# Two of three token groups share the weight chunks of an output projection in a two-layer encoder kernel

## The chip, the cores and the metric

The kernel runs on one core of a Trainium2 chip. The metric is the device time of one execution in microseconds (us). The engines of a core are TensorE (PE; PEld is its weight load), VectorE (DVE), ScalarE (ACT), GpSimd (POOL) and SyncE (SP), which here issues nearly all DMAs.

## What is computed

An encoder trunk of two layers and a final RMSNorm, on a prompt of 1024 tokens and a sample of 512, width 1024, in float32. Cut to what matters:

```python
def attn_retention_layer(x, g, w_in, qk_gain, ret_decay, w_out):      # layer 0
    z = rmsnorm(x, g) @ w_in
    ...        # oa: attention over all tokens, 8 heads on 2 kv heads; ob: retention, 4 heads
    mixed = jnp.concatenate([jax.nn.silu(ga) * oa, jax.nn.silu(gb) * ob], axis=-1)
    return x + mixed @ w_out

def windowed_layer(x, g, w_in, sink, rel_bias, w_out):                # layer 1
    ...        # o: attention in a window of +-128 tokens, 16 heads on 2 kv heads
    return x + (jax.nn.silu(gate) * o) @ w_out

def trunk(x, ...):
    x = attn_retention_layer(x, ...)
    x = windowed_layer(x, ...)
    return rmsnorm(x, final_norm)
```

`trunk` is applied to the prompt and to the sample with the same weights. The change concerns the two lines `x + ... @ w_out`.

## The kernel before

**Groups and operands.** The 12 blocks of 128 tokens form three groups of 512 (`NG`, `GB`): t=0 and t=1 are the prompt's halves, t=2 is the sample. The order of work is `ORDER = (2, 0, 1)`. Each float32 operand of a projection is held as a high and a low part (`split`: high part on ACT, low part on DVE), and one step of a projection is three matmuls, high by high, low by high and high by low. The width of 1024 is cut into eight slices of 128, numbered k; `X["h", k, t]` and `X["l", k, t]` are the parts of slice k of group t.

**Weights.** `load_w` (L130) loads one chunk of 256 output columns: four DMAs of 256 KB into raw buffers (two in all), for each a copy to the high part on POOL (L136) and a subtraction for the low part (L137) on POOL or, where `lo` is given, on DVE. Parts go into four buffers of the tag "w" or four of the tag "wg". The "wg" buffers also serve `stage` (L250), from which come the tiles of the mixes (`mo`), of the residual (`y`), of the reloaded rows (`yn`) and of the norm (`dg`).

**Two forms of output projection.** `out_proj_fm` (L263) works with features on the partitions and the weights stationary: per chunk two blocks of 128 features, each 8 steps k of three matmuls 128x512. Behind each block come the residual add on DVE (L278), a store of the result to memory, the square on ACT (L280) and the accumulation on POOL (L282). At its end matmuls with ones give the sums of squares and a tile `R` that holds the row factors of the norm for every partition (L288 to L295), and a last pass reloads every stored block and finishes it (`fin`, L301): in layer 0 by `fin_fm` (L804: multiplication on POOL, then `split_x`), in layer 1 by `fin_out` (L1006: one DVE step and the output store). `out_proj` (L316) works with tokens on the partitions: per chunk four blocks of tokens, each 8 steps of three matmuls 128x256, the residual add in place (L326); it loads its own weights with high priority, odd chunks into "wg" buffers. Its finish is `fin_ab` (L842: norm per block, transposes, splits) or `fin_c` (L1033: norm per block on ACT, POOL and DVE, and stores).

**The mixes.** `mix_fm` (L254) makes the input of a projection: it loads an attention output and a gate, multiplies them on POOL (L259) and splits the product. The last slices of a group are mixed directly at the end of their attention unit (`Back.mix`, L661).

**What sets the order.** Attention A and attention C run through `pipeline` (L673), unit by unit (group of heads, token block), group t=2 first; the scores of later units run beside the products of the current one. After every key block the pipeline calls `fill.step()`, which advances a generator of other work by a rate (`Fill`, L229; `FillC`, L899); a step is three matmuls. `hook_a` (L810) and `hook_c` (L1012) are called once per unit and put output projections into the filler as soon as their group's attention is complete: in both layers t=2 at the first unit of t=0, then t=0 at the first unit of t=1; inside the projection each block advances the mixes of the next group by one (`ahead`). The projection of t=1 follows after attention as `out_proj`. So each of the two output weights is loaded three times. A scheduler that simulates a timeline (L1129) then orders the instructions of each engine within the data's dependencies and the priorities.

## Time and profile before

| | |
|---|---|
| runs, us | 1539.06, 1546.78, 1547.49; median 1546.78 |
| span of the profiled execution, us | 1541.9 |
| PE busy | 1467.9 us, 95% |
| PEld, DVE, ACT, POOL busy | 83%, 69%, 46%, 52% |
| DMA | 179.54 MB, mean 116 GB/s |
| out weights | 48 loads of 256 KB for layer 0, 48 for layer 1 |

The span holds, in this order: input projections and retention, attention A with filler (to 831 us), the rest of projection AB (to 875 us), the projections and attention C with filler (to 1429 us), projection C and the final norm. A share of busy time is a mean over all of these. A busy PE is counted with overlaps, since matmuls are pipelined; the price of one in a row is read from the chain of waits.

### The profile page before, as it was taken

The page shows a single profiled execution, that of the slowest core. Times are in us where ns is not written, and L with a number is a line of the kernel's source. Part 1 is how long each engine was busy: PE and PEld are TensorE (multiplying, and loading weights), DVE is VectorE, ACT ScalarE, POOL GpSimd, SP SyncE. Part 2 cuts the span into 40 slices and gives each one's busy share as a digit, 9 for nine tenths or more (in the row PEclk, how much of TensorE's full clock was granted, in tenths as well). Part 3 has the DMA queues.
Part 4 walks back from the last instruction along what each step waited for, and adds up shares of the span by engine and source line. Part 5 has one row for each costly group of instructions (what it writes and reads, how often), then busy time and mean ns, then how long its engine had stood idle before and what let it go on. Part 6 is the DMA issues. An engine that isn't in the chain of part 4 may idle for free.

```text
span 1541.9 us, 26034 instructions
## 1 busy us (share of the span) xinstructions
PE 1467.9 (95%) x8746; PEld 1277.2 (83%) x8746; DVE 1061.1 (69%) x2488; ACT 714.0 (46%) x1768; POOL 804.7 (52%) x1040
## 2 busy tenths in 40 slices
PE   7989999989999999999998999999999999988897
PEld 7988999987888888778777998888888888766677
DVE  6596455578667667877888327677777767898554
ACT  3632222245455555655653235556556556555102
POOL 7783334257456374887896414442522432567433
PEclk9998999999999999999999999999999999999999
DMA  9441011224421132654563422112213211567773
GB/s 334 155 154 52 19 45 49 64 85 140 138 73 59 48 110 73 217 166 130 153 218 115 124 78 78 52 57 56 80 49 93 61 53 52 169 211 235 242 247 123
DMA packets 112662, 179.54 MB, mean 116 GB/s; under 512 B 12880, under 2 KB 34000, under 8 KB 112528
## 3 DMA queue, kind: packets, MB, share of 16 engines
q1 hardware_dynamic: 110512, 172.37, 35.6%
q0 software_dynamic: 2016, 5.51, 1.2%
q8 instruction: 69, 1.13, 0.3%
q14 instruction: 65, 0.53, 0.1%
HBM read 125.63 MB, written 56.39 MB: 118 GB/s over the span
## 4 chain that ended last, share of the span: by engine, by line
PE 65%; DVE 12%; DMA 8%; POOL 5%; issue 4%; ACT 2%; SPq 1%; POOLq 0%; DVEq 0%; ACTq 0%
PE psg L89 16%; PE psq L89 10%; PE psb L89 8%; PE po L89 8%; PE pte L170 6%; PE pso L89 4%; PE sc L89 3%; PE s L89 3%; PE pskv L89 2%; DMA wraw<-in_woc 2%; DVE xl L118 1%; DVE w L137 1%; DVE nm L782 1%; DMA wraw<-in_woab 1%; DVE el L112 1%
## 5 line engine op out<-in xcount | busy, mean ns | idle before, releaser
L89 PE MATMUL psg<-xh,wg 128*128 128x512 f32 x768 | 261.6, 399 | 1.4 <-POOL wg L137 1.2
L112 DVE TENSOR_TENSOR el<-pte,eh 128x512 fp32r<-128x512 f32 x288 | 196.6, 684 | 56.7 <-ACT eh L111 29.6
L107 POOL TENSOR_SCALAR ec<-ec,rl 128x384 f32<-128x384 f32 (+1 forms) x192 | 109.0, 582 | 233.0 <-DVE rl L997 77.1
L111 ACT ACTIVATE eh<-pte 128x512 fp32r<-128x512 f32 x288 | 169.4, 596 | 119.6 <-PE po L89 66.4
L89 PE MATMUL pso<-xh,w 128*128 128x512 f32 x512 | 179.8, 409 | 9.8 <-DVE w L137 4.3
L89 PEld LDWEIGHTS psg<-xh,wg 128*128 128x128 f32 x768 | 143.7, 188 | 29.7 <-POOL wg L137 1.6
L107 POOL TENSOR_SCALAR e<-e,rl 128x512 f32<-128x512 f32 x160 | 114.6, 728 | 81.7 <-DVE rl L793 23.8
L89 PE MATMUL psg<-xl,wg 128*128 128x512 f32 x384 | 151.1, 393 | 0.0
L992 ACT ACTIVATE ec<-ec,nm 128x384 f32<-128x384 f32 (+1 forms) x192 | 109.6, 572 | 85.6 <-DVE nm L990 80.8
L790 ACT ACTIVATE e<-s,nm 128x512 f32<-128x512 f32 x160 | 108.9, 687 | 75.3 <-DVE nm L787 56.1
L136 POOL TENSOR_SCALAR w<-wraw 128x512 fp32r<-128x512 f32 x116 | 78.7, 680 | 117.7 <-DMA wraw<-in_woc 35.2
L782 DVE TENSOR_REDUCE nm<-s 128x1 f32<-128x512 f32 x160 | 107.5, 682 | 34.3 <-PE s L89 34.0
L89 PE MATMUL psq<-xh,w 128*128 128x512 f32 x384 | 130.1, 397 | 0.6 <-DVE oT L655 0.6
L89 PEld LDWEIGHTS pso<-xh,w 128*128 128x128 f32 x512 | 96.1, 191 | 34.7 <-DVE w L137 7.8
L986 DVE CUSTOM_DVE_ANT_0 ec<-sc,bias,sink_s 128x384 f32<-128x384 f32 (+1 forms) x192 | 105.2, 568 | 20.3 <-PE sc L89 17.4
L89 PE MATMUL pso<-xl,w 128*128 128x512 f32 x256 | 102.0, 399 | 3.3 <-DVE xl L118 3.3
L170 PEld LDWEIGHTS pte<-ident,e 128*128 128x128 f32 x640 | 78.4, 142 | 20.5 <-ACT e L790 1.7
L170 PE MATMUL pte<-ident,e 128*128 128x128 f32 x640 | 94.6, 275 | 0.8 <-ACT e L790 0.6
L137 POOL TENSOR_TENSOR w<-wraw,w 128x512 fp32r<-128x512 f32 x68 | 90.5, 1335 | 1.8
L89 PEld LDWEIGHTS psq<-xh,w 128*128 128x128 f32 x384 | 71.8, 188 | 14.4 <-PE po L89 0.9
L89 PEld LDWEIGHTS psg<-xl,wg 128*128 128x128 f32 x384 | 72.3, 188 | 13.2
L89 PE MATMUL pskv<-w,xh 128*128 128x256 f32 x384 | 73.3, 293 | 9.0 <-ACT xh L117 6.7
(225 smaller groups left out, 3981.8 us busy)
## 6 DMA issues: line engine op xcount, KB each, us to landing
wraw<-in_woab SPq DMA_DIRECT2D x48, 256.0 KB, 3.3
wraw<-in_woc SPq DMA_DIRECT2D x48, 256.0 KB, 3.6
wraw<-in_wab SPq DMA_DIRECT2D x44, 256.0 KB, 3.3
wraw<-in_wc SPq DMA_DIRECT2D x36, 256.0 KB, 3.2
xt<-in_xT SPq DMA_DIRECT2D x24, 256.0 KB, 5.3
xb<-in_x SPq DMA_DIRECT2D x24, 256.0 KB, 4.9
qd<-qdw SPq DMA_DIRECT2D x24, 256.0 KB, 2.0
qd<-qd SPq DMA_DIRECT2D x24, 256.0 KB, 3.1
```

Source lines behind the costliest of these rows:

```text
L89: i = nc.tensor.matmul(ps, lhsT=lhsT, rhs=rhs, start=start, stop=stop)
L107: nc.gpsimd.tensor_scalar(o, i, s, 1.0, ALU.mult, ALU.mult)
L111: nc.scalar.activation(hi, src, AF.Copy)
L112: nc.vector.tensor_tensor(lo, src, hi.bitcast(F32), ALU.subtract)
L118: nc.vector.scalar_tensor_tensor(lo, src, scale, hi.bitcast(F32), ALU.mult, ALU.subtract)
L136: nc.gpsimd.tensor_scalar(w[:, 0, :], raw, 1.0, 1.0, ALU.mult, ALU.mult)
L137: (lo or nc.gpsimd).tensor_tensor(w[:, 1, :], raw, w[:, 0, :].bitcast(F32), ALU.subtract)
L170: return nc.tensor.transpose(o, i, ident)
L782: nc.vector.tensor_reduce(nm2[:, c:c + 1] if nh == 2 else nm[:, h:h + 1], s, AX.X, ALU.max, negate=True)
L790: nc.scalar.activation(eh[c], ss[c], AF.Exp, bias=nm[:, h:h + 1], accum_out=l[:, h, c:c + 1])
L986: nc.vector.tensor_tensor_reduce(es[h][:, :nk], s, bias[h][:, bo:bo + nk], 1.0, sink_s[:, 4 * c + h:4 * c + h + 1], ALU.add, ALU.max, mx[: ...
L992: nc.scalar.activation(es[a][:, :nk], es[a][:, :nk], AF.Exp, bias=nm[:, a:a + 1], accum_out=l[:, a:a + 1])
```

## The change

Only the sample's output projection (t=2) remains filler, in attention A at a rate of 1.15 in place of 2.00. After attention a new function, `out_proj_both`, works on both prompt groups: for each chunk it loads the weights once, with high priority and the low part on DVE, projects two feature blocks of t=0 with weights stationary, then four token blocks of t=1. The results of t=0 stay on the chip until their finish (`ybuf`); in layer 0 they are also stored, as residual for layer 1, in layer 1 they aren't. The norm's sums for t=0 are made after the last chunk's first token block, and the finish of all eight blocks of t=0 (`finish0`) is written ahead of the finish of t=1. The mixes of t=0 and t=1 stay tied to the filler blocks (`aside`), what is left of them is drained at the end of attention. The loads of out weights fall from 48 to 32 per layer.

```diff
+RATE_O = 1.15
...
+    ahead = []
+    def aside():
+        while ahead:
+            if next(ahead[0], aside) is not aside:
+                return
+            ahead.pop(0)
+    def drain():
+        while ahead:
+            aside()
+    def fm_block(w, a, t, k, ks, y, sq, acc, ps):
+        nc.vector.tensor_tensor(y, ps, y, ALU.add)
+        nc.scalar.activation(sq if k else acc, y, AF.Square)
+        if k:
+            nc.gpsimd.tensor_tensor(acc, acc, sq, ALU.add)
+    def fm_rstd(acc, dg, one, rb):
+        nc.gpsimd.memset(one, 1.0)
+        ps = ps_s("ssq")
+        for j in range(GB):
+            mm(ps[:, j:j + 1], acc[:, j * P:(j + 1) * P], one[:, 0:1], True, True)
+        r = rstd_of(ps[:, :GB], D, GB)
+        ps = ps_s("R")
+        for j in range(GB):
+            nc.vector.tensor_scalar(dg[:, j * P:(j + 1) * P], ident, r[:, j:j + 1], None, ALU.mult)
+            mm(ps[:, j * P:(j + 1) * P], one, dg[:, j * P:(j + 1) * P], True, True)
+        nc.scalar.activation(rb, ps, AF.Copy)
...
                     if kk != ks[-1]:
                         yield
-                for side in ahead[:1] + (prev or []):
-                    next(side, None)
-                nc.vector.tensor_tensor(y, ps, y, ALU.add)
+                aside()
+                fm_block(w, a, t, k, ks, y, sq, acc, ps)
                 dma(out=dst[k][t], in_=y)
-                nc.scalar.activation(sq if k else acc, y, AF.Square)
-                if k:
-                    nc.gpsimd.tensor_tensor(acc, acc, sq, ALU.add)
                 yield
...
-        def fin():
-            for k in range(KT):
-                y = stage("yn")[0] if prev is None else buf("Q", "yn")
-                dma(out=y, in_=dst[k][t])
-                finish(t, k, y, rb)
-                yield
-        if prev is None:
-            late.append(fin())
-        else:
-            yield from fin()
-
-    late, ahead = [], []
-
-    def drain(gens):
-        while gens:
-            for _ in gens.pop():
-                pass
-
-    def out_proj(t, warr, ks, res, finish):
-        x1 = [load_block(res(t * GB + j), "xr") for j in range(GB)]
+        for k in range(KT):
+            y = stage("yn")[0]
+            dma(out=y, in_=dst[k][t])
+            finish(t, k, y, rb)
+            yield
+    def out_proj_both(warr, ks, ybuf, res0, keep, finish0, res1, finish1):
+        acc = buf("T", "acc")
+        ys, x1 = [], []
+        def weights(c):
+            with tc.high_priority():
+                return load_w(warr, c, "wg" if c % 2 else "w", nc.vector, None, ks)
+        w = weights(0)
         for c in range(4):
-            with tc.high_priority():
-                w = load_w(warr, c, "wg" if c % 2 else "w", nc.vector, None, ks)
+            for a in range(2):
+                k = 2 * c + a
+                y = ybuf(k)
+                dma(out=y, in_=res0(k))
+                ps = ps_any("pso")
+                for kk in ks:
+                    proj_fm_k(ps, w, a * P, 0, kk, ks)
+                fm_block(w, a, 0, k, ks, y, buf("H", "sq"), acc, ps)
+                keep(k, y)
+                ys.append(y)
+            nxt = weights(c + 1) if c < 3 else None
+            if c == 0:
+                x1 = [load_block(res1(GB + j), "xr") for j in range(GB)]
             for j in range(GB):
                 ps = ps_any("pso")[:, :CW]
-                proj_tm(ps, w, t * GB + j, ks)
+                proj_tm(ps, w, GB + j, ks)
                 sl = x1[j][c // 2][:, (c % 2) * CW:(c % 2 + 1) * CW]
                 with tc.high_priority():
                     nc.vector.tensor_tensor(sl, ps, sl, ALU.add)
-        finish(t, x1)
+                if (c, j) == (3, 0):
+                    rb = buf("T", "rb")
+                    fm_rstd(acc, buf("H", "dg"), buf("O", "one", P), rb)
+            w = nxt
+        for k in range(KT):
+            finish0(0, k, ys[k], rb)
+        finish1(1, x1)
...
     def hook_a(u):
         g, b = u
-        if g == 1 and b in (BLOCKS[GB], BLOCKS[2 * GB]):
-            t = 2 if b == BLOCKS[GB] else 0
-            if t == 2:
-                late.clear()
-                fill.rest()
-                fill.rate = 2.00
-            drain(ahead)
-            if t:
-                drain([mix_fm(t, KS_A, o_ab, g_ab)])
-            ahead.append(mix_fm(0 if t else 1, KS_A[:6], o_ab, g_ab))
-            fill.gens.append(out_proj_fm(t, woab, KS_A, lambda k: xT[k][:, t * 512:(t + 1) * 512], x1T_d, fin_fm,
-                                         None if t else late, None))
+        if g == 1 and b == BLOCKS[GB]:
+            fill.rest()
+            fill.rate = RATE_O
+            ahead.append(mix_fm(2, KS_A, o_ab, g_ab))
+            drain()
+            ahead.append(mix_fm(0, KS_A[:6], o_ab, g_ab))
+            fill.gens.append(out_proj_fm(2, woab, KS_A, lambda k: xT[k][:, 2 * 512:3 * 512], x1T_d, fin_fm, None))
+        if g == 1 and b == BLOCKS[2 * GB]:
+            ahead.append(mix_fm(1, KS_A[:6], o_ab, g_ab))
 
...
-    out_proj(1, woab, KS_A, lambda b: x[b], fin_ab)
+    pairs = {}
+    def y_ab(k):
+        if k >= 6:
+            return buf("S2", "y2")
+        if k % 2 == 0:
+            pairs[k // 2] = buf("S4", "y4")
+        return pairs[k // 2][:, (k % 2) * 512:(k % 2 + 1) * 512]
+    out_proj_both(woab, KS_A, y_ab, lambda k: xT[k][:, 0:512], lambda k, y: dma(out=x1T_d[k][0], in_=y), fin_fm,
+                  lambda b: x[b], fin_ab)
...
     def hook_c(u):
         c, b = u
-        if c == 3 and b in (BLOCKS[GB], BLOCKS[2 * GB]):
-            t = 2 if b == BLOCKS[GB] else 0
+        if c == 3 and b == BLOCKS[GB]:
             for _ in fillc.gates:
                 pass
-            if t == 2:
-                late.clear()
-            drain(ahead)
-            drain([mix_fm(t, KS_C if t else KS_C[6:], o_c, g_c)])
-            ahead.append(mix_fm(0 if t else 1, KS_C[:6], o_c, g_c))
-            fillc.more.append(out_proj_fm(t, woc, KS_C, lambda k: x1T_d[k][t], x2T_d, fin_out, None if t else late, nc.vector))
+            ahead.append(mix_fm(2, KS_C, o_c, g_c))
+            drain()
+            ahead.append(mix_fm(0, KS_C[:6], o_c, g_c))
+            fillc.more.append(out_proj_fm(2, woc, KS_C, lambda k: x1T_d[k][2], x2T_d, fin_out, nc.vector))
+        if c == 3 and b == BLOCKS[2 * GB]:
+            ahead.extend([mix_fm(0, KS_C[6:], o_c, g_c), mix_fm(1, KS_C[:6], o_c, g_c)])
 
...
-    out_proj(1, woc, KS_C, lambda b: x1_d[b], fin_c)
+    out_proj_both(woc, KS_C, lambda k: buf("Q", "y"), lambda k: x1T_d[k][0], lambda k, y: None, fin_out,
+                  lambda b: x1_d[b], fin_c)
```

On POOL at the end of attention A, before (w and wg are weights, acc the sums of squares, yn the reloaded rows, mo a mix, oT an attention output):

```order
L282 TENSOR_TENSOR acc<-acc,y 128x512
L136 TENSOR_SCALAR w<-wraw 128x512
L282 TENSOR_TENSOR acc<-acc,y 128x512
L136 TENSOR_SCALAR wg<-wraw 128x512 x3
L103 TENSOR_TENSOR rstd<-ms,nhalf 128x4
L136 TENSOR_SCALAR wg<-wraw 128x512
L805 TENSOR_TENSOR yn<-yn,rb 128x512 x7
L666 TENSOR_TENSOR oT<-oT,gq 128x256
L136 TENSOR_SCALAR w<-wraw 128x512 x2
```

and after:

```order
L104 TENSOR_TENSOR rstd<-ms,nhalf 128x4
L697 TENSOR_TENSOR oT<-oT,gq 128x256
L836 TENSOR_TENSOR yn<-yn,rb 128x512 x8
L281 TENSOR_TENSOR acc<-acc,sq 128x512
L260 TENSOR_TENSOR mo<-mo 128x512
L697 TENSOR_TENSOR oT<-oT,gq 128x256
L284 MEMSET one 128x128
L260 TENSOR_TENSOR mo<-mo 128x512
L137 TENSOR_SCALAR wg<-wraw 128x512
L260 TENSOR_TENSOR mo<-mo 128x512
L137 TENSOR_SCALAR wg<-wraw 128x512
L260 TENSOR_TENSOR mo<-mo 128x512
```

The eight multiplications `yn` (now the sample's) are followed by mixes of group 1, which before had been made earlier, between filler blocks.

On PE at the same place, before (po is the last product of attention A, pso the projection of group 1, xh and xl the parts of one of its slices):

```order
L89 MATMUL pso_10142<-w_10056,xh71_9755 128x256
L89 MATMUL po_9796<-el_9904,av_7802 128x512
L89 MATMUL pso_10142<-w_10056,xh71_9755 128x256
L89 MATMUL pso_10142<-w_10056,xl71_9756 128x256
L89 MATMUL pso_10214<-wg_10170,xh01_9074 128x256 x2
L89 MATMUL pso_10214<-wg_10170,xl01_9075 128x256
L89 MATMUL pso_10214<-wg_10170,xh11_9216 128x256 x2
L89 MATMUL pso_10214<-wg_10170,xl11_9217 128x256
```

and after:

```order
L90 MATMUL po_9457<-eh_9555,av_7799 128x512
L90 MATMUL po_9457<-el_9556,av_7799 128x512
L90 MATMUL pso_9741<-w_9625,xh01_9243 128x256 x2
L90 MATMUL pso_9741<-w_9625,xl01_9244 128x256
L90 MATMUL pso_9741<-w_9625,xh11_9396 128x256 x2
L90 MATMUL pso_9741<-w_9625,xl11_9397 128x256
L90 MATMUL pso_9741<-w_9630,xh41_9594 128x256 x2
L90 MATMUL pso_9767<-w_9630,xh41_9594 128x256 x2
L90 MATMUL pso_9793<-w_9630,xh41_9594 128x256 x2
L90 MATMUL pso_9741<-w_9630,xl41_9595 128x256
L90 MATMUL pso_9767<-w_9630,xl41_9595 128x256
L90 MATMUL pso_9793<-w_9630,xl41_9595 128x256
```

The number behind a name's h or l tells slice and group: xh41 is the high part of slice 4 of group 1, which comes from the first of the mixes above. Before, the first chunk of group 1 ended beside the last product, one tile after the other, and its second chunk followed; now most of the first chunk stands behind the last product, slice by slice through three tiles.

On DVE at the end of the program, before (xr is a token block of group 1, L326 its residual add, L1037 its last scaling):

```order
L1037 SCALAR_TENSOR_TENSOR xr_17608<-xr_17608,rstd,fn 128x512
L326 TENSOR_TENSOR xr_17612<-pso,xr_17612 128x256
L181 TENSOR_REDUCE ssum<-ss 128x1
L100 TENSOR_SCALAR ms<-ssum 128x1
L1037 SCALAR_TENSOR_TENSOR xr_17612<-xr_17612,rstd,fn 128x512
L326 TENSOR_TENSOR xr_17616<-pso,xr_17616 128x256
L181 TENSOR_REDUCE ssum<-ss 128x1
L100 TENSOR_SCALAR ms<-ssum 128x1
L1037 SCALAR_TENSOR_TENSOR xr_17616<-xr_17616,rstd,fn 128x512
```

and after:

```order
L1073 SCALAR_TENSOR_TENSOR xr_17236<-xr_17236,rstd,fn 128x512
L182 TENSOR_REDUCE ssum<-ss 128x1
L101 TENSOR_SCALAR ms<-ssum 128x1
L1073 SCALAR_TENSOR_TENSOR xr_17240<-xr_17240,rstd,fn 128x512
L1045 SCALAR_TENSOR_TENSOR y<-y,g_sb,rb 128x512 x8
L351 TENSOR_TENSOR xr_17244<-pso,xr_17244 128x256
L182 TENSOR_REDUCE ssum<-ss 128x1
L101 TENSOR_SCALAR ms<-ssum 128x1
L1073 SCALAR_TENSOR_TENSOR xr_17244<-xr_17244,rstd,fn 128x512
```

Eight finishing steps of group 0 (L1045) now stand ahead of the residual add of the last token block.

## Rows read from the trace of the kernel before

**Rows 1.** The page's busy times: engine, microseconds, share of the span, instructions.
```profile
PE 1467.9 (95%) x8746; PEld 1277.2 (83%) x8746; DVE 1061.1 (69%) x2488; ACT 714.0 (46%) x1768; POOL 804.7 (52%) x1040
```

**Rows 2.** Windows: length, busy PE, PEld, DVE, ACT, POOL (instructions), clock, DMA share, GB/s.
```profile
390.00:620.00 230.00, 228.85 (x1171) 189.12 (x1170) 150.36 (x314) 122.13 (x274) 126.34 (x157) 1.00 0.27 81
622.00:831.00 209.00, 198.10 (x1022) 159.04 (x1021) 171.55 (x312) 116.68 (x260) 168.10 (x176) 0.99 0.56 172
1336.00:1429.00 93.00, 81.69 (x379) 63.14 (x379) 84.30 (x178) 46.90 (x117) 66.10 (x71) 0.98 0.69 222
```

**Rows 3.** Waits of PE's weight loads, 635.6 to 809.8: total, times, longest.
```profile
PEld s L89 <- ACT e L790: 3.4, 3, 2.7
...
PEld pte L170 <- issue: 0.2, 1, 0.2
```

**Rows 4.** Timeline of ACT: start, length, evacuation of a unit's accumulator, three units.
```profile
635.64 0.60 ACT L650 ACTIVATE olo<-po 64x512 f32<-64x512 f32 x1
809.82 0.59 ACT L650 ACTIVATE olo<-po 64x512 f32<-64x512 f32 x1
1429.12 0.59 ACT L650 ACTIVATE olo<-po 64x512 f32<-64x512 f32 x1 [3.08 <-PE po L89]
```

**Rows 5.** Windows of the three stretches that are costed, columns as in rows 2.
```profile
635.60:809.80 174.20, 168.12 (x847) 134.62 (x846) 143.68 (x264) 100.96 (x228) 147.38 (x156) 0.99 0.56 171
809.80:875.10 65.30, 58.69 (x440) 55.83 (x439) 40.42 (x68) 19.05 (x45) 36.56 (x39) 0.97 0.40 120
1429.10:1532.40 103.30, 95.20 (x583) 82.98 (x582) 56.67 (x91) 14.54 (x34) 38.85 (x46) 0.97 0.66 207
```

**Rows 6.** The chain of waits: start, length, matmuls of 256 and of 512 columns.
```profile
889.30 26.75 PE pskv L89 x223
936.20 5.49 PE psg L89 x24
```

**Rows 7.** Groups of DVE, 635.6 to 809.8: busy, mean ns, idle before.
```profile
L792 DVE TENSOR_TENSOR rl<-l 128x1 f32<-128x1 f32 x28 | 14.9, 533 | 7.6 <-ACT e L790 7.4
L118 DVE SCALAR_TENSOR_TENSOR xl<-mo,xh 128x512 fp32r<-128x512 f32 x15 | 14.9, 992 | 5.1 <-ACT xh L117 5.0
L278 DVE TENSOR_TENSOR y<-pso,y 128x512 f32<-128x512 f32 x14 | 9.5, 680 | 0.4 <-PE pso L89 0.4
```

**Rows 8.** Groups of POOL in the same stretch.
```profile
L137 POOL TENSOR_TENSOR w<-wraw,w 128x512 fp32r<-128x512 f32 x28 | 38.6, 1380 | 0.3
L136 POOL TENSOR_SCALAR w<-wraw 128x512 fp32r<-128x512 f32 x29 | 18.6, 643 | 6.7 <-PE pso L89 5.2 <-DMA wraw<-in_woab 1.3
L259 POOL TENSOR_TENSOR mo<-mo 128x512 f32<-128x512 f32 x14 | 18.1, 1292 | 4.9 <-DMA mo<-gab 2.5 <-PE pte L170 2.2 <-DMA mo<-oab 0.2
L282 POOL TENSOR_TENSOR acc<-acc,y 128x512 f32<-128x512 f32 x12 | 17.3, 1440 | 5.2 <-DVE rl L793 5.2
L805 POOL TENSOR_TENSOR yn<-yn,rb 128x512 f32<-128x512 f32 x8 | 10.8, 1345 | 2.1 <-DMA yn<-x1T 2.1
```

**Rows 9.** Timeline of POOL at the end of attention A.
```profile
831.33 11.46 POOL L805 TENSOR_TENSOR yn<-yn,rb 128x512 f32<-128x512 f32 x7
```

**Rows 10.** DMA issues on the page: count, KB each, median microseconds to landing.
```profile
wraw<-in_woab SPq DMA_DIRECT2D x48, 256.0 KB, 3.3
```

**Rows 11.** Waits of PE's weight loads in projection C, 1429.1 to 1532.4.
```profile
PEld pso L89 <- POOL w L136: 8.4, 6, 2.5
PEld pso L89 <- DVE w L137: 3.4, 8, 1.0
```

**Rows 12.** Groups of DVE, 1429 to the end.
```profile
L1007 DVE SCALAR_TENSOR_TENSOR yn<-yn,g_sb,rb 128x512 f32<-128x512 f32 x16 | 12.3, 792 | 2.3 <-DMA yn<-x2T 1.2 <-issue 1.1
```

**Rows 13.** Timeline of DVE at the end of the program.
```profile
1533.65 1.74 DVE L1037 SCALAR_TENSOR_TENSOR xr<-xr,rstd,fn 128x512 f32<-128x512 f32 x1 [0.67 <-POOL rstd L103]
1535.32 0.41 DVE L326 TENSOR_TENSOR xr<-pso,xr 128x256 f32<-128x256 f32 x1
```

**Rows 14.** Groups of DVE, 390 to 620.
```profile
L792 DVE TENSOR_TENSOR rl<-l 128x1 f32<-128x1 f32 x31 | 7.9, 254 | 13.5 <-ACT e L790 13.3
```

More of the change, by code (lines that the diff above doesn't have):

```diff
@@ L261, in mix_fm, with out_proj_fm @@
             yield
-    def out_proj_fm(t, warr, ks, res, dst, finish, prev, lo):
+    ahead = []
[23 more added lines that the diff above has]
+        nc.scalar.activation(rb, ps, AF.Copy)
+    def out_proj_fm(t, warr, ks, res, dst, finish, lo):
         acc = buf("T", "acc")
@@ L286, in out_proj_fm @@
-        ps = ps_s("ssq")
-        for j in range(GB):
-            mm(ps[:, j:j + 1], acc[:, j * P:(j + 1) * P], one[:, 0:1], True, True)
-        r = rstd_of(ps[:, :GB], D, GB)
-        ps = ps_s("R")
-        for j in range(GB):
-            nc.vector.tensor_scalar(dg[:, j * P:(j + 1) * P], ident, r[:, j:j + 1], None, ALU.mult)
-            mm(ps[:, j * P:(j + 1) * P], one[:, :P], dg[:, j * P:(j + 1) * P], True, True)
         rb = buf("T", "rb")
-        nc.scalar.activation(rb, ps, AF.Copy)
+        fm_rstd(acc, dg, one[:, :P], rb)
```

9 lines of the change are left out of this document (4 added, 5 removed).

## The prediction

> **What bounds the kernel now.** I read the page's busy times first: TensorE (PE) is busy for 95% of the span, far ahead of VectorE (DVE, 69%), GpSimd (POOL, 52%) and ScalarE (ACT, 46%) [rows 1]. The change leaves the number of matmuls and their sizes as they are, so it can win only where PE waits now, and it loses wherever it makes PE wait anew. Next I cut the span into stages. While attention A is filled with gate projections (390 to 620 us) PE is busy for 228.85 of 230 us and DVE for 0.65 of the time; while it is filled with output projections (622 to 831 us) DVE rises to 0.82 and POOL to 0.80; at the end of attention C, DVE is at 0.91 and PE falls to 0.88 [rows 2]. So the stages with projection filler are where PE is not the only engine near its limit. The list of waits for the seven units of attention A that carry the filler has 11 rows, 13.5 us in all, led by waits for exponentials and splits [rows 3]. The evacuations of the unit accumulator mark the stage: the last sample unit ends at 635.64, the last but one unit at 809.82, and attention C's last unit at 1429.12 [rows 4]. The three stretches to be costed are then 174.2 us (seven units), 65.3 us (from there to the last matmul of projection AB) and 103.3 us (from the end of attention C to the last matmul of projection C) [rows 5].
>
> **Prices.** On the chain of waits, where PE runs without a gap, 24 matmuls of 512 columns take 5.49 us, 0.229 each, and 223 of 256 columns 26.75 us, 0.120 each [rows 6]. The durations in the lists of lines are longer since neighbours overlap, so I don't sum those. A group that is projected with stationary weights needs 8 blocks of 24 matmuls of 512 columns, 44.0 us; the token-major group needs 384 of 256 columns, 46.1 us.
>
> **1. Attention A gets less filler.** By the order of instructions, 128 of group 0's matmuls leave these seven units: 128 x 0.229 = 29.3 us. (Twelve matmuls of 256 columns come in and twelve transposes go, which cancels.) With the waits of 13.5 us [rows 3] held, the stretch goes from 174.2 to 145 us: **-29**. All of this work comes back in step 2. Whether the waits hold is the open point. DVE was busy 143.7 of 174.2 us [rows 5]. It loses, for the group 0 blocks, six adds of 0.68 us and some of the mixes and splits that are now made later (0.99 us each) [rows 7], about 11 us, and would have 132 us of work in 145, a share of 0.91. That is just the share at which attention C already runs [rows 2], so I take the wait as unchanged, and no gain on top. POOL loses far more: of 29 copies of 0.64 us and 28 subtractions of 1.38 us [rows 8] roughly half, besides five accumulations of 1.44: about 36 us, to some 111 of 145.
>
> The Trainium skill, page "Perfetto Trace Analysis", section "Identifying the Most-Contended Engine", would have TensorE judged by the busy share of its weight loads and the others by occupancy. Between 622 and 831 us that is 159.04 of 209 for the loads, 0.76, below DVE's 0.82, so by this rule taking PE work out of the stage buys little. This supports the slower rival below; the 0.95 of matmul time and the 13.5 us of waits speak against it.
>
> **2. End of attention A and projection AB.** Now the stretch is 65.3 us. Moved here are the 29.3 us of step 1, and one new stall. At the end of the last but one unit the sample's R row becomes ready, and POOL's queue then holds, in this order, eight multiplications for the sample's finish, an accumulation and four mixes of group 1, where before the mixes came earlier, beside filler. Before, POOL needed 11.46 us for seven such multiplications [rows 9], with a mean of 1.35 each [rows 8]. From the evacuation: R about +1, its copy +2, eight times 1.35 and a load's delay to +14, an accumulation of 1.44 and a mix of 1.29 [rows 8], then ACT's and DVE's split: PE can begin with the first of these mixes at about +17. Ahead of it PE has only the last unit's remaining transposes and products, some 7 us, so it idles for about **10 us**. The mixes follow at 1.3 to 2 us and the last is there at +24; what is left of chunk 0 then takes 51 x 0.12 = 6 us, to +30. Chunks 1 to 3 need 2 x 24 x 0.229 + 96 x 0.120 = 22.5 us each, and the four loads of a chunk at 3.3 us [rows 10] fit in this. With 2% of small waits: +99.5. Net **+34** against 65.3. Of this 29 is the moved work and 5 the stall, less the 5 us and more that PE waited here before.
>
> **3. Removed loads.** 32 of the 96 weight transfers of 256 KB go, with their copies and subtractions, and the stores and reloads of group 0. In layer A those were hidden by matmuls already, so alone they bring 0. I bound the input projection of layer C, which follows, at -2 to +4 (group 1's transposes start with the same blocks as before) and take 0.
>
> **4. Layer C.** Its filler for group 0 mostly runs after attention already. By the order only 24 matmuls (5.5 us) move out of attention; with DVE at 0.91 there not all of that time is saved: **-4**. After attention there are now 168 matmuls of 512 columns and 384 of 256: 84.6 us of work in 103.3, so PE idles 18.7; 8.4 and 3.4 us of it are waits for the weight copies and subtractions [rows 11], since a token-major chunk of 11.5 us needs four loads of 3.3 and their two conversions. Afterwards a chunk is 22.5 us of work for the same four loads, and these waits should go. There are 90.1 us of work, and I allow 4.5 for chunk 0, which waits for mixes that come after attention, and 2% for the rest: 97. That is -6, **-10** with the 4 above.
>
> **5. The end of the program.** In the order DVE's eight finishing steps of group 0 (y by gain and R) now stand between the last block but one and the last block's residual add. They take 0.79 us each [rows 12]: 6.3 us. Before, that add ran at 1535.32, right behind one finishing step of 1.74 [rows 13], and 6.6 us from there the span ended. The steps can begin only when the step for the block before is through, so most of them is exposed: **+5** (0 if R is ready early and the scheduler's order leaves a gap to hide them, +8 if the eight stores of 256 KB also hold up the last ones).
>
> **Sum**: -29 + 34 + 0 - 10 + 5 = 0 on the profiled span of 1541.9. The median of the runs, 1546.78, lies 4.9 us above that span, so the forecast is **1547 us**. About 0.5%, 7.7 us, is what a measurement of this kernel tells from no change.
>
> **Rivals.**
> (a) *Faster: attention A's waits fall with the load of POOL and DVE.* The pair add of the softmax sums takes 533 ns in the filled units [rows 7] and 254 ns before them [rows 14], and a split 0.99 us; if POOL's smaller share shortens these again, DVE has 28 x 0.28 = 8 us less, some 15 with the splits, and is at 0.87. Then PE's waits go most of the way to those of 390 to 620 us, where it was idle for 1.15 of 230 [rows 2]: with 3.5 us of them left the units take 135 instead of 145, -10. The same shortens the chain of multiplications in step 2 by 4, and in C chunk 0 waits for nothing, -5. In all -19: **1528 us**. The Trainium skill, page "SBUF — State Buffer", section "Who interferes with whom", says the same of the cause: VectorE's instructions with two SBUF inputs and GpSimd's reads exclude each other for whole instructions. The 533 and 254 ns agree with it, though they don't show it alone.
> (b) *Slower: DVE bounds the seven units.* If it can't be filled to more than the 143.7 / 174.2 = 0.825 it has now, its 132 us take 160 instead of 145, +15: **1562 us**. This decides as soon as DVE's waits are latency between engines rather than idleness for lack of PE results; the three waits for exponentials [rows 3] speak for it, attention C's 0.91 [rows 2] against.
> (c) *The sharing doesn't free PE.* Odd chunks go through the four buffers that mixes, staged rows and weights share. If their loads wait until mixes of group 1 are read, 3 us for each of two odd chunks in each layer, PE waits 12 us more than I have: **1559 us**. For it speaks that the first odd chunk is loaded just when the mixes are late (step 2); against, that chunk 0's work covers a load of 3.3 us.
>
> **Chances.** Forecast (within 0.5%) 0.37, (a) 0.33, (b) 0.22, (c) 0.08. Faster by over 0.5% is (a), 0.33; slower is (b) and (c), 0.30. The range goes from (a) with 3 us for an end of the program that costs less, to (b) with 3 more for the stores: 1525 to 1565.
>
> **What would show it.** Right: units of attention A at 20.7 us each; a PE gap of about 10 us between the last product of attention A and the first of the late mixes, with POOL's eight multiplications in it; chunks 1 to 3 of either layer at 22.5 us; waits for weights in layer C's projection down from 12 us to 4 or less; some 14 us from the last projection matmul to the end of the span. Units near 23 us would be (b), near 19.3 (a). If the weight waits in C stay, or odd chunks begin late, it is (c). What would make the forecast wrong most easily is the size of step 1's wait, since 29 us of PE work are taken out of a stage in which DVE is then as full as PE.

## The result

The changed kernel is slower: 1557.53 us in the median of four runs (1551.24 to 1558.83) against 1545.07 (1539.06 to 1547.49), a ratio of 1.0083, 95% interval 1.0055 to 1.0112. That lies in the range of the prediction, but outside the half per cent around its forecast of 1547. The profiled execution was the fastest of the four. The page of the changed kernel, its first lines (as [rows 1]):

```profile
span 1549.5 us, 25836 instructions
...
PE 1466.7 (95%) x8746; PEld 1279.0 (83%) x8746; DVE 1031.5 (67%) x2472; ACT 713.9 (46%) x1768; POOL 761.7 (49%) x992
```

PE has the same work, VectorE 30 us less and GpSimd 43 us less; so the whole loss is time in which PE waits or runs slowly. To find it I cut both traces at the same marks: the evacuation of the last sample unit, that of the last but one unit of attention A, the last matmul of projection AB, the last of layer C's key and value projection, the last evacuation of attention C, the last matmul of projection C, the end. The evacuations in the changed kernel, timeline of ScalarE (as [rows 4]):

```profile
633.98 0.59 ACT L681 ACTIVATE olo<-po 64x512 f32<-64x512 f32 x1
...
781.22 0.59 ACT L681 ACTIVATE olo<-po 64x512 f32<-64x512 f32 x1 [0.81 <-PE po L90]
...
1429.41 0.59 ACT L681 ACTIVATE olo<-po 64x512 f32<-64x512 f32 x1 [0.21 <-DVE oT L686]
```

The stretches between the marks, windows of the changed kernel (length, busy PE, PEld, DVE, ACT, POOL, granted clock, DMA share, GB/s, as [rows 5]):

```profile
634.00:781.20 147.20, 136.05 (x710) 108.53 (x709) 120.96 (x250) 87.96 (x207) 94.45 (x109) 1.00 0.40 123
781.20:886.70 105.50, 95.51 (x584) 84.16 (x584) 43.77 (x72) 26.61 (x57) 51.16 (x52) 0.90 0.39 125
886.70:925.30 38.60, 38.45 (x324) 38.25 (x323) 19.40 (x29) 17.37 (x43) 17.66 (x15) 1.00 0.08 25
925.30:1429.40 504.10, 494.34 (x2523) 414.24 (x2522) 380.40 (x1128) 287.28 (x778) 214.02 (x303) 1.00 0.32 100
1429.40:1536.60 107.20, 97.57 (x606) 88.05 (x605) 41.40 (x76) 18.96 (x46) 38.87 (x40) 0.95 0.37 112
1536.60:1549.50 12.90, 0.05 (x1) 0.00 (x0) 7.71 (x13) 1.66 (x4) 1.01 (x2) 0.66 0.70 261
```

And the three stretches of the kernel before that stand in no row above, in windows:

```profile
875.40:916.10 40.70, 38.75 (x322) 38.31 (x323) 8.16 (x21) 12.15 (x35) 9.71 (x15) 1.00 0.15 46
916.10:1429.10 513.00, 500.77 (x2547) 418.32 (x2546) 390.70 (x1136) 290.27 (x784) 223.82 (x311) 1.00 0.32 100
1532.60:1541.90 9.30, 0.06 (x1) 0.00 (x0) 3.45 (x7) 2.97 (x9) 2.33 (x3) 0.72 0.37 139
```

Beside the prediction's steps, in us (marks read to 0.1 us):

| stretch | before | after | difference | predicted |
|---|---|---|---|---|
| seven units of attention A | 174.2 | 147.2 | -27.0 | -29 |
| rest of attention A and projection AB | 65.4 | 105.5 | +40.1 | +34 |
| key and value projection of C | 40.7 | 38.4 | -2.3 | 0 |
| rest of layer C to the end of attention | 513.2 | 504.3 | -8.9 | -4 |
| projection C | 103.4 | 107.1 | +3.7 | -6 |
| to the end | 9.4 | 13.0 | +3.6 | +5 |
| sum from the last sample unit on | 906.3 | 915.5 | +9.2 | 0 |

Up to the first mark the two kernels issue nearly the same work, and the changed one was there 1.7 us earlier (the last section shows how far runs spread there); this is why the span differs by 7.6 and not by 9.2.

**The end of attention A.** Windows of the changed kernel where PE loses time, at the end of attention A and behind attention C:

```profile
781.20:805.00 23.80, 15.61 (x69) 10.94 (x69) 19.95 (x26) 14.49 (x26) 18.98 (x16) 0.68 0.70 230
805.00:830.00 25.00, 23.20 (x129) 20.31 (x128) 11.93 (x17) 2.32 (x4) 8.93 (x10) 0.90 0.35 96
1429.40:1450.00 20.60, 15.60 (x80) 13.25 (x79) 10.52 (x19) 4.89 (x11) 11.36 (x12) 0.88 0.64 200
1450.00:1475.00 25.00, 22.06 (x123) 19.50 (x124) 12.66 (x19) 2.25 (x4) 7.26 (x8) 0.89 0.67 213
```

From 781 to 805 us PE executes 69 instructions; from 805 to 830 it executes 129. What is ahead of it there, on GpSimd (timeline; the bracket is the idle time before and what ended it):

```profile
784.09 3.85 POOL L836 TENSOR_TENSOR yn<-yn,rb 128x512 f32<-128x512 f32 x3 [0.54 <-ACT rb L293]
788.61 1.27 POOL L836 TENSOR_TENSOR yn<-yn,rb 128x512 f32<-128x512 f32 x1 [0.67 <-DMA yn<-x1T]
791.25 1.57 POOL L836 TENSOR_TENSOR yn<-yn,rb 128x512 f32<-128x512 f32 x1 [1.37 <-DMA yn<-x1T]
793.10 4.74 POOL L836 TENSOR_TENSOR yn<-yn,rb 128x512 f32<-128x512 f32 x3 [0.28 <-DMA yn<-x1T]
797.80 1.71 POOL L281 TENSOR_TENSOR acc<-acc,sq 128x512 f32<-128x512 f32 x1
799.48 1.72 POOL L260 TENSOR_TENSOR mo<-mo 128x512 f32<-128x512 f32 x1
```

The eight multiplications of the sample's finish and then the first late mix, in the predicted order. On VectorE at the same time (timeline), the split of a sample row (L119) stands ahead of each low part (L113) that the last unit's products need:

```profile
786.73 0.68 DVE L113 TENSOR_TENSOR el<-pte,eh 128x512 fp32r<-128x512 f32 x1
787.33 1.16 DVE L119 SCALAR_TENSOR_TENSOR xl<-yn,g_sb,xh 128x512 fp32r<-128x512 f32 x1
788.42 0.68 DVE L113 TENSOR_TENSOR el<-pte,eh 128x512 fp32r<-128x512 f32 x1
789.02 1.41 DVE L119 SCALAR_TENSOR_TENSOR xl<-yn,g_sb,xh 128x512 fp32r<-128x512 f32 x1
```

The waits of PE's weight loads from 781.2 to 830 us (total, times, longest), first the products, then the late mixes:

```profile
PEld po L90 <- DVE el L113: 7.4, 6, 1.8
PEld pso L90 <- ACT xh L118: 5.5, 4, 3.3
```

With two smaller entries these are 13 short waits, 15.3 us in all, where one gap of about 10 us was predicted. By PE's timeline the chunks 1, 2 and 3 begin at 817.7, 840.1 and 862.5 us: the first of them 36.5 us behind the mark, where 30 were predicted, and then 22.4 apart, where 22.5 were. The whole excess is in chunk 0.

**Projection C.** The waits for weights of [rows 11] are gone (0.3 us remain); these stand in their place, from 1429.4 to 1536.6:

```profile
PEld pso L90 <- ACT xh L118: 8.7, 4, 3.0
PEld pso L90 <- DVE y L278: 2.1, 2, 1.5
```

The xh are high parts of late mixes, and GpSimd, which makes the mixes, waits for their loads (timeline):

```profile
1443.57 1.26 POOL L260 TENSOR_TENSOR mo<-mo 128x512 f32<-128x512 f32 x1 [4.35 <-DMA mo<-gc]
...
1453.73 1.27 POOL L260 TENSOR_TENSOR mo<-mo 128x512 f32<-128x512 f32 x1 [2.77 <-DMA mo<-gc]
```

The loads of the last two mixes were issued at 1450.3 and 1451.2 us, right behind the landings of two stores of the sample's rows (1450.3 and 1451.0), which use the same buffers. Chunk 1 begins at 1465.1 us, 35.7 behind the mark, where 27 were allowed for chunk 0.

### The profile page after: what moved, and what is told of

Its sections match the earlier page's. It is cut to its first block, busy times and chain, and to the rows that moved or that the text cites. A ratio compares the mean times of both kernels' runs of the same rounds, so it can differ in the third digit from the quotient of the medians.

```text
span 1549.5 us, 25836 instructions
## 1 busy us (share of the span) xinstructions
PE 1466.7 (95%) x8746; PEld 1279.0 (83%) x8746; DVE 1031.5 (67%) x2472; ACT 713.9 (46%) x1768; POOL 761.7 (49%) x992
## 3 DMA queue, kind: packets, MB, share of 16 engines
q1 hardware_dynamic: 102448, 157.69, 32.1%
## 4 chain that ended last, share of the span: by engine, by line
PE 69%; DVE 11%; POOL 5%; DMA 4%; issue 3%; ACT 2%; SPq 0%; POOLq 0%; DVEq 0%; ACTq 0%
PE psg L90 16%; PE psq L90 10%; PE pso L90 10%; PE psb L90 8%; PE po L90 8%; PE pte L171 6%; PE sc L90 3%; PE s L90 3%; DVE xl L119 1%; PE pskv L90 1%; DVE nm L813 1%; DMA wraw<-in_woc 1%; DVE el L113 1%; POOL mo L260 1%; DVE qdw L431 1%
## 5 line engine op out<-in xcount | busy, mean ns | idle before, releaser
L113 DVE TENSOR_TENSOR el<-pte,eh 128x512 fp32r<-128x512 f32 x288 | 196.4, 684 | 57.4 <-ACT eh L112 29.1
L90 PE MATMUL pso<-xh,w 128*128 128x512 f32 x384 | 136.3, 405 | 2.6 <-DVE w L138 1.4
L1024 DVE CUSTOM_DVE_ANT_0 ec<-sc,bias,sink_s 128x384 f32<-128x384 f32 (+1 forms) x192 | 105.2, 568 | 21.8 <-PE sc L90 18.6
L137 POOL TENSOR_SCALAR w<-wraw 128x512 fp32r<-128x512 f32 x84 | 56.2, 669 | 77.1 <-PE pskv L90 23.3
L90 PEld LDWEIGHTS pso<-xh,w 128*128 128x128 f32 x384 | 72.6, 190 | 17.3 <-DVE w L138 1.9
L171 PE MATMUL pte<-ident,ec 128*128 128x128 f32 x512 | 78.8, 273 | 2.0 <-POOL ec L108 1.9
L90 PE MATMUL pso<-xl,w 128*128 128x512 f32 x192 | 76.2, 397 | 1.9 <-DVE xl L119 1.9
```

The source lines that it names most:

```text
L90: i = nc.tensor.matmul(ps, lhsT=lhsT, rhs=rhs, start=start, stop=stop)
L113: nc.vector.tensor_tensor(lo, src, hi.bitcast(F32), ALU.subtract)
L137: nc.gpsimd.tensor_scalar(w[:, 0, :], raw, 1.0, 1.0, ALU.mult, ALU.mult)
L171: return nc.tensor.transpose(o, i, ident)
L1024: nc.vector.tensor_tensor_reduce(es[h][:, :nk], s, bias[h][:, bo:bo + nk], 1.0, sink_s[:, 4 * c + h:4 * c + h + 1], ALU.add, ALU.max, mx[: ...
```

## The experiments

All stretches in us, read from each trace at the same marks; "A" is the seven units, "AB" the rest to the last matmul of projection AB, "kv" the key and value projection, "C" the rest of layer C to the end of attention, "pC" projection C, "end" the end. The ratio is to the kernel before, with its 95% interval.

| kernel | A | AB | kv | C | pC | end | sum | ratio |
|---|---|---|---|---|---|---|---|---|
| before | 174.2 | 65.4 | 40.7 | 513.2 | 103.4 | 9.4 | 906.3 | |
| changed | 147.2 | 105.5 | 38.4 | 504.3 | 107.1 | 13.0 | 915.5 | 1.0083 (1.0055 to 1.0112) |
| e1 layer A alone | 148.7 | 105.8 | 38.4 | 511.0 | 101.9 | 9.4 | 915.1 | 1.0068 (1.0043 to 1.0093) |
| e2 layer C alone | 174.3 | 64.7 | 40.9 | 506.6 | 106.9 | 13.6 | 907.1 | 1.0007 (0.9992 to 1.0022) |
| e3 early mixes | 150.5 | 93.5 | 38.4 | 510.0 | 98.3 | 13.0 | 903.8 | 0.9979 (0.9963 to 0.9995) |
| e4 finish written last | 148.7 | 105.2 | 38.4 | 502.6 | 106.8 | 13.0 | 914.8 | 1.0077 (1.0047 to 1.0107) |
| e5 early mixes, finish held | 149.4 | 86.9 | 38.4 | 511.0 | 97.0 | 13.0 | 895.8 | 0.9955 (0.9941 to 0.9970) |
| e6 early mixes, not shared | 146.5 | 107.6 | 39.5 | 511.7 | 115.2 | 13.0 | 933.6 | 1.0168 (1.0150 to 1.0185) |
| e7 early mixes, rate 1.60 | 167.0 | 84.0 | 38.4 | 511.5 | 98.1 | 13.0 | 912.1 | 1.0050 (1.0034 to 1.0066) |
| e8 e5, finish split | 148.7 | 87.1 | 38.4 | 510.5 | 96.9 | 14.6 | 896.1 | 0.9953 (0.9938 to 0.9968) |
| e9 e5, blocks forward | 151.4 | 87.1 | 39.1 | 512.2 | 96.8 | 12.7 | 899.2 | 0.9938 (0.9914 to 0.9962) |
| e10 finish held alone | 153.7 | 90.4 | 38.4 | 505.2 | 100.0 | 13.0 | 900.7 | 0.9965 (0.9947 to 0.9982) |
| e11 e9, rate 1.40 | 156.1 | 87.6 | 39.2 | 512.5 | 97.5 | 12.7 | 905.6 | 0.9993 (0.9978 to 1.0008) |
| e12 e9, finish spread | 149.0 | 86.9 | 39.1 | 510.4 | 97.2 | 12.0 | 894.6 | 0.9912 (0.9892 to 0.9932) |

**Which layer loses: e1 and e2.** Each has the new function in one layer, and in the other the old pair with its old hook. The lines are e1's; e2 does the same in layer A.

```diff
-    out_proj_both(woc, KS_C, lambda k: buf("Q", "y"), lambda k: x1T_d[k][0], lambda k, y: None, fin_out,
-                  lambda b: x1_d[b], fin_c)
+    old_proj(1, woc, KS_C, lambda b: x1_d[b], fin_c)
```

> Only projection AB is changed as in the new kernel; layer C stays as in the kernel before. Theory 1 (the traces add up by stretch): attention A's end is where the loss is. In the two traces the new kernel stands 9.2 us behind when the key and value projection of layer C ends and the later stretches give 1.6 back, so this kernel should be about 9 us slower than before (ratio 1.006). Theory 2 (the loss is in layer C's projection and the end of the program, which became 7 us longer in the traces, and layer A's part is given back in layer C): within 2 us of before.

> Only projection C is changed as in the new kernel; layer A stays as in the kernel before. Theory 1: attention C ends 8.8 us earlier relative to its start, the projection takes 3.8 and the end of the program 3.4 us more, so -2 us (ratio 0.999). Theory 2 (the loss sits here): +7 us, ratio 1.005.

Measured: 1.0068 and 1.0007, from the last sample unit on +8.8 and +0.8 us, together 9.6 where both parts at once give 9.2. The parts add up, and layer A carries the loss. In e1 Theory 1 stands, and the 40 us in AB are there unchanged. e2 was to be 2 us faster and isn't, but it is far from the 7 us of Theory 2.

**Whether the late mixes are it: e3.**

```diff
                 aside()
+                aside()
                 fm_block(w, a, t, k, ks, y, sq, acc, ps)
```

> The new kernel with two mixes in place of one for each filler block, so that in layer A none and in layer C two of group 1's mixes are left for the time after attention. Theory 1 (late mixes are what PE waits for at the end of both attentions: 19.3 us of PE waiting from 781 to 830 and 15.2 after 1429 in the new kernel's trace): 8 us less at the end of attention A and 7 less in projection C than the new kernel, so about 1543 us, no slower than before. Theory 2 (at the end of attention A the sample's eight finishing multiplications and splits hold PE up, whether mixes are behind them or not; in projection C the weights take the place of the mixes): at most 4 us less than the new kernel.

Measured: 1541.01 us, 0.9979, as Theory 1 gave, about 16 us below the changed kernel's median. By stretches 3.3 of the 12.0 us that AB gains are lost again in the seven units, into which the mixes went, and in layer C 5.7 of 8.8 in attention; 11.7 remain. Waits were left in e3. At the end of attention A the products still wait for low parts, weight loads from 784.5 to 881 us:

```profile
PEld po L90 <- DVE el L113: 5.2, 4, 2.6
```

and in projection C, from 1429.8 to 1528.2, the first odd chunk is late:

```profile
PEld pso L90 <- POOL wg L137: 4.8, 1, 4.8
```

GpSimd could not copy these weights because the sample's rows, reloaded for their finish, still held the "wg" buffers until they were stored: the first two copies start at 1456.3 and 1457.5 us, 0.2 behind the landings of two of the rows' stores (1456.1 and 1457.3), while their data had landed by 1443.2. That is the mechanism of rival (c), with the sample's rows in the place of mixes; the changed kernel itself doesn't show it since it waits for mixes first.

**The sample's finish: e10 alone, e5 with early mixes.** The reloaded rows of the sample are written behind the first shared chunk, in buffers of the attention's exponentials.

```diff
-            y = stage("yn")[0]
-            dma(out=y, in_=dst[k][t])
-            finish(t, k, y, rb)
-            yield
+        late.append(fin())          # the same four lines with y = buf("E", "yn")
@@ out_proj_both, at the end of each chunk
+            while late:
+                for _ in late.pop():
+                    pass
```

> The new kernel with one mix for a filler block, as it was, and only the sample's finish moved behind the first shared chunk, in buffers of its own. Theory A (at the end of attention A it is the sample's eight multiplications and splits ahead of the mixes that PE waits for): layer A gains as much as in e5, layer C's late mixes stay, so 8 to 10 us less than the new kernel, 1547 to 1549 if before is 1544. Theory B (it is the number of mixes left that counts): at most 3 us less than the new kernel, ratio 1.006 or more.

> The kernel with early mixes (e3), and besides the finish of the sample's rows written behind the first shared chunk in both layers, in buffers that the odd weight chunks don't use. Theory: what is left of the loss is that the sample's rows share buffers and VectorE with what PE waits for: in e3 the first odd chunk of layer C waits 4.8 us until such rows are stored, and the last products of attention A wait 5.2 us for splits that stand behind the sample's. So 5 us less than e3 (about 1536 us), 10 if both go. Rival: the waits of that size in e3 only mask loads that come no sooner, and the time stays within 2 us of e3 (1541).

Measured: e10 0.9965, e5 0.9955. In e10 layer A (A and AB) takes 244.1 us, 8.6 less than the changed kernel, with not one more mix called for in the source: the scheduler placed all of group 1's mixes of layer A ahead of the end of attention (the last at 763.7 us, the mark is at 790.1). That the rows no longer took the buffers that the mixes need is the likely reason; no run tests it alone. So theory B is out, and theory A holds only in part: layer A gains half of e5's 16.4 us, and layer C, where the late mixes were to stay, gains 6.2 in its two stretches (one wait of 5.4 us for a late mix is left there). Since the mixes moved too, e10 doesn't separate the finish from them. e3 alone gives 8.7 in layer A, both together 16.4. In e5 the same place runs without a gap; windows, and GpSimd's timeline, where the multiplications now begin 12 us behind the mark in place of 3:

```profile
786.70:812.00 25.30, 25.30 (x156) 22.20 (x154) 15.82 (x21) 12.09 (x21) 14.71 (x11) 1.00 0.52 165
```

```profile
798.87 5.52 POOL L848 TENSOR_TENSOR yn<-yn,rb 128x512 f32<-128x512 f32 x4 [8.06 <-DMA yn<-x1T]
```

In 25.3 us PE executes 156 instructions at a granted clock of 1.00, where the changed kernel had 69 in 23.8 us at 0.68. Layer A is then 3.3 us shorter than before, layer C's two stretches 8.6.

**Is it the sharing that pays: e6.** As e3, but each chunk is loaded twice, once for each group.

```diff
+            w = weights(c, "wg")
-            nxt = weights(c + 1) if c < 3 else None
+            nxt = weights(c + 1, "w") if c < 3 else None
```

> The kernel with early mixes (e3), but each chunk's weights are loaded twice behind attention, once for group 0 and once for group 1, so nothing is shared and only the place of the projections is changed. Theory 1 (sharing is what makes the chunks of 22.5 us run without waits for weights): eight loads of 3.3 us for a chunk are 26 us, 4 us more than the matmuls, so 20 to 30 us slower than e3 over both layers. Theory 2 (two loads in flight hide each other, sharing brings nothing to PE): within 3 us of e3.

Measured: 1567.97 us, 27 more than e3 (29.8 by the stretches), the number of Theory 1. But its reason holds only in part. Projection C takes 16.9 us more, and it has one wait of 13.6 us where e3's was 4.8, the list of waits from 1438 to 1553 us:

```profile
PEld pso L90 <- POOL wg L137: 13.6, 1, 13.6
```

and it is again a buffer that the sample's rows hold (GpSimd's timeline):

```profile
1464.53 0.62 POOL L137 TENSOR_SCALAR wg<-wraw 128x512 fp32r<-128x512 f32 x1 [9.53 <-DMA out_s<-yn]
```

Layer A's two stretches take 10.1 us more; the longest wait there, 4.6 us, is again for a copy into "wg". So sharing is worth a good deal in this arrangement, but how much of it would be left with buffers of their own was not tried.

**What bounds attention A's units: e7 and e11.**

```diff
-RATE_O = 1.15
+RATE_O = 1.60      # e7, on e3; 1.40 in e11, on e9
```

> The kernel with early mixes (e3) with the sample's projection at a rate of 1.60 in place of 1.15 in attention A: it ends about two units earlier, its finish falls into attention, and the last units run without filler. Theory 1 (the seven units are bound by matmuls): the units with filler grow to 23 us, those without fall to about 16, and the 8.5 us of PE waiting at the end of attention A in e3 shrink, in all 3 to 6 us less than e3. Theory 2 (without filler a unit is bound by VectorE and by latency): those units stay at 18 us or more, PE waits in them, and the kernel is 3 to 6 us slower than e3.

> As e9 with the sample's projection at a rate of 1.40 in place of 1.15. In e7 the units that ran out of filler still took 20.8 to 25 us for 12 us of PE work, so attention A's units have a floor that isn't PE's. Theory (units of about 21 us have room for some 20 us of PE work and hold 17.5 at the rate 1.15): at 1.40 the early units stay within 1 us of 21 and the last ones take group 0's first blocks instead, 3 to 6 us less than e9. Rival (group 0's blocks don't come forward, as in e7): 3 us or more slower than e9.

Measured: 1549.59 and 1542.53 us, each 8 us slower than its base: the direction of Theory 2 with a larger size, and the rival in e11. Windows of e7, a unit with filler and two that have nearly none:

```profile
709.50:731.90 22.40, 21.57 (x112) 17.27 (x111) 18.81 (x40) 13.58 (x33) 15.46 (x18) 1.00 0.44 128
...
759.50:784.70 25.20, 17.89 (x81) 13.54 (x82) 20.86 (x40) 15.34 (x32) 17.30 (x16) 0.86 0.22 68
784.70:805.50 20.80, 15.32 (x85) 11.99 (x84) 17.88 (x36) 11.62 (x27) 12.18 (x15) 0.92 0.48 135
```

With 81 and 85 PE instructions in place of 112 the units take 25.2 and 20.8 us in place of 22.4; at 1.15 they take 21. That looks like a floor of the unit, but isn't shown to be one. The sample's finish runs through both: the longest waits of PE's weight loads there, 3.4 and 3.0 us, are for low parts that stand behind the sample's splits on VectorE, as at the end of attention A in the changed kernel. In e11, where the finish is held, the unit that ran out of filler took 15.2 us, behind one of 25.9 with 153 PE instructions (windows of e11):

```profile
775.40:790.60 15.20, 13.07 (x76) 9.95 (x77) 11.90 (x30) 11.24 (x29) 6.19 (x9) 1.00 0.33 106
```

By the stretches e11 loses 6.4 us to e9: its seven units take 4.7 more, 4.1 of them busy time of PE, and what came forward didn't shorten AB, where PE waits 3.5 us in one piece behind the last unit's output. So a higher rate loses in both kernels; what bounds the units stays open.

**The end of the program: e4, e8, e9, e12.** In the changed kernel, on VectorE's timeline, the eight steps of group 0 and the residual add behind them:

```profile
1537.54 5.38 DVE L1045 SCALAR_TENSOR_TENSOR y<-y,g_sb,rb 128x512 f32<-128x512 f32 x8
1542.84 0.41 DVE L351 TENSOR_TENSOR xr<-pso,xr 128x256 f32<-128x256 f32 x1
```

```diff
-        for k in range(KT):                         # e4: behind finish1, in layer C alone
-            finish0(0, k, ys[k], rb)
         finish1(1, x1)
+        for k in range(KT):
+            finish0(0, k, ys[k], rb)
@@ e8: fin_out
+        if t == 0 and k % 2:
+            nc.gpsimd.tensor_tensor(y, y, rb, ALU.mult)
+            nc.scalar.activation(y, y, AF.Copy, scale=gk)
@@ e9: the token blocks of each chunk
+                if (c, j) == (2, 1):
+                    blocks(3, nxt)                  # group 0's last two feature blocks
@@ e12: the finish of group 0
+            if step is not None and k >= 4:
+                tc.add_manual_dep(step.ins, add.ins.name, order, reason="behind the last residual add")
```

> The new kernel with group 0's eight finishing steps of layer C written behind group 1's finish in place of ahead of it. If those eight steps ahead of the last residual add are what lengthens the end of the program (13.0 us from the last projection matmul to the end in place of 9.5), the end falls back to about 9.5 and the kernel is 3.5 us faster than the new one. Rival: the eight output stores of 256 KB then come last and the end stays within 1 us of 13.

> As e5, and every second finishing step of group 0 at the end of layer C on GpSimd and ScalarE in place of VectorE. Theory (the eight steps of 0.66 us ahead of the last residual add lengthen the end of the program): four of them less are 2.6 us less than e5, about 1533 us if e5 gives 1536, 0.7% faster than the kernel before. Rival (GpSimd's four multiplications of 1.3 us hold up the last norm in their turn): no gain against e5.

> As e5 (early mixes, the sample's finish behind the first shared chunk in its own buffers), and group 0's last two feature blocks in the middle of the third chunk instead of ahead of the fourth, so that its norm is known 17 us before the last projection matmul. Theory (what lengthens the end of the program is that group 0's eight finishing steps come too late to lie beside matmuls): from the last projection matmul to the end about 9.5 us in place of 13, and 3.5 us less than e5 in all, about 1531 us, 0.993 of before. Rival (the stores or group 1's own chain set the end): 13 us stay, no gain.

> As e9, and the last four of group 0's eight finishing steps held behind the last residual add by an order on VectorE. In e9 the norm of group 0 was known early, but the eight steps stood together for 5.4 us ahead of the last two adds, and 12.5 us from the last projection matmul to the end stayed. Theory (it is the place of the eight steps in VectorE's queue, not when they could begin): from the last projection matmul to the end about 10 us, 2.5 less than e9. Rival (the output stores set the end): 12.5 us stay.

Measured, from the last matmul to the end: 13.0, 14.6, 12.7 and 12.0 us. e4 tells nothing of the end: the scheduler put the eight steps ahead of the last add as before, wherever they were written. The order of instructions in its trace is that of the changed kernel on every engine, so it is a second profile of that kernel, and tells how far a stretch differs between two profiles: by up to 1.7 us (C). In e8 the rival holds, for a reason it didn't name; VectorE's four steps, and GpSimd's four beside them (two timelines):

```profile
1517.79 6.75 DVE L1062 SCALAR_TENSOR_TENSOR y<-y,g_sb,rb 128x512 f32<-128x512 f32 x4
```

```profile
1517.28 6.71 POOL L1059 TENSOR_TENSOR y<-y,rb 128x512 f32<-128x512 f32 x4
```

Four steps take 6.75 us beside GpSimd, 1.69 each, where eight took 5.38 alone, 0.67 each. The Trainium skill, page "SBUF — State Buffer", section "Who interferes with whom", says that a VectorE instruction with two inputs from SBUF and a GpSimd instruction that reads SBUF exclude each other; these two rows agree. e9 didn't do what it was to do: group 0's row factors (`rb`) were there 2.8 us ahead of the last projection matmul, in place of 0.5 in e5 and the expected 17, so it doesn't test its theory, and the norm was not known early, as the expectation of e12 has it. The steps still stood in one row ahead of the last two adds. In e12 they are spread (VectorE's timeline):

```profile
1518.87 2.73 DVE L1065 SCALAR_TENSOR_TENSOR y<-y,g_sb,rb 128x512 f32<-128x512 f32 x4
1521.53 0.74 DVE L364 TENSOR_TENSOR xr<-pso,xr 128x256 f32<-128x256 f32 x2
1522.19 3.73 DVE L1065 SCALAR_TENSOR_TENSOR y<-y,g_sb,rb 128x512 f32<-128x512 f32 x4
```

That gives 0.7 us against e9, not the expected 2.5: the later four now stand ahead of the last blocks' sums. The eight steps are certainly in the chain, but no run brought the end back to 9.4 us, so that nothing else holds it is not shown.

e12 has the lowest median: 1532.22 us in six runs, 0.9912 of before, and so faster than both kernels. Its interval overlaps that of e9, and only 0.7 of the 4.6 us between them lie at the end, so that it beats e9 is not shown.

## Why the prediction was right or wrong

**Step 1, the seven units: right in size, its mechanism open.** -27.0 against -29. The waits were to hold, and VectorE to be the knife edge at 0.91. But PE's busy time fell by 32.1 us (168.1 to 136.1), more than the 29.3 of the step, and its idle time rose by 5.1, so that part of the agreement is luck. VectorE was busy for 121.0 of 147.2 us, 0.82, since rival (a)'s relief did come: the pair adds fell from 533 ns [rows 7] to 241, in the groups of VectorE from 634 to 781.2:

```profile
L823 DVE TENSOR_TENSOR rl<-l 128x1 f32<-128x1 f32 x27 | 6.5, 241 | 11.4 <-ACT e L821 11.4
```

But the rival's next step failed. PE's waits didn't fall with it, they rose from 13.5 us to 19.6 (a list of ten rows, the largest here):

```profile
PEld s L90 <- issue: 5.5, 2, 3.3
```

What holds the units isn't shown. VectorE's share stayed at the 0.82 of before, as in rival (b), whose bound with the smaller work gives 121.0 / 0.825 = 146.7 us, an estimate near the measured 147.2; but in the last two of the seven units PE is busy for 20.91 of 21.5 and for all of 20.4 us. The first rule weighed in step 1, from the Trainium skill's page "Perfetto Trace Analysis", section "Identifying the Most-Contended Engine", was read there as speaking against this gain. 27.0 us of the 29.3 taken out came, but VectorE's work fell by 22.7 us as well, so this trace doesn't decide on the rule.

**Step 2, the end of attention A: right cause, too small a size.** Forecast +34, measured +40.1; this is the first step that failed, in its term for chunk 0, which ended 36.5 us behind the mark and not 30. GpSimd's eight multiplications ended at +16.6 us in place of +14, since three loads were late, and the mixes reached PE at about +21 in place of +17. What the step left out is VectorE's queue. It let PE run the last unit's 7 us of work freely ahead of the stall, but the low parts of these products stood behind the sample's splits (7.4 us of waits). And it priced the matmuls behind the stall at full speed; the granted clock was 0.68 and then 0.90 in these windows. How the 6.1 us divide between queue and clock no run separates. e3, e10 and e5 show the cause: with the finish and the mixes out of the way AB is 18.6 us shorter than in the changed kernel, and layer A as a whole 16.4.

**Step 3, the key and value projection: near.** -2.3, just below its bounds of -2 to +4.

**Step 4, layer C: wrong by 5.** Forecast -10, measured -5.2. The waits for weights went as predicted, from 11.8 us to 0.3. But I allowed 4.5 us for late mixes, and they cost 8.7, as their loads share buffers and queue with the sample's rows; with 2.1 for residual adds and a clock of 0.88 to 0.89 up to 1475 us projection C became longer by 3.7, not shorter by 6. The gain in attention was larger than forecast, 8.9 in place of 4, of which 6.4 are less busy time of PE and the rest less waiting. With the causes gone (e5) the two stretches give -8.6, near the forecast.

**Step 5, the end: right**, +3.6 against +5.

**The sum.** 0 was forecast, +9.2 measured: 6 from step 2, 5 from step 4, 2 from step 1, less 2 in step 3 and 1 in step 5. So "no measurable change" failed on two terms of the sum that have one root, the late mixes behind the sample's finish. The range holds the measured time only because two rivals that did not happen drew it up to 1565. (b) gives a time near the measured one but not its place, since the units took 147 and not 160 us; (c), at 1559 us the nearest, was not what the changed kernel waited for (0.3 us), and came out, with the sample's rows in the way, only once the mixes were early.

## What to carry to other kernels

When filler is thinned, follow what rode on it: here the next group's mixes were tied to filler blocks and slid to the one place where nothing covered them. Price the moved step on every engine's queue that it passes, VectorE's as well as GpSimd's, and look at whose buffers its tiles take. And when a unit is run without filler to see its floor, make sure that nothing else passes through its queues: in e7 the sample's finish did.

## What the runs showed of the hardware

Runs of the same work differ by several microseconds ahead of the first mark: the changed kernel evacuates the last sample unit at 633.98 us, and e4, with the same order on every engine, at 640.13. All 14 profiled executions lie between 632.6 and 640.1. One place where they part is the start. From 20 to 30 us the changed kernel ran at a granted clock of 1.00, with 82 matmuls (window):

```profile
20.00:30.00 10.00, 9.88 (x82) 9.89 (x83) 6.00 (x11) 3.66 (x9) 9.17 (x12) 1.00 1.04 388
```

and e4 at a mean of 0.71, with 61:

```profile
20.00:30.00 10.00, 9.82 (x61) 9.83 (x62) 5.20 (x10) 2.44 (x6) 8.22 (x10) 0.71 1.04 388
```

A mean between the two levels of 1.2 and 2.4 GHz says that part of the window ran at the lower one. In both PE had been busy for less than 11 of the 20 us before. So times of single profiles are best counted from a mark behind the start, as in the tables above.
